# Measured durations and a DMA clock in a planner of instruction order, and block merges that alternate between halves of the TensorE array

## Chip, cores and metric

One Trainium2 chip, one core, one launch. The metric is the device time in microseconds (us) of the whole launch. Engines are named as in the profile: PE (TensorE), ACT (ScalarE), DVE (VectorE), POOL (GpSimd), SP (SyncE, which issues the DMAs).

## The reference

Two blocks of a sequence model on 512 tokens of width 2048, all in fp32. Block 1 projects the normed input, runs a gated delta rule of 24 heads in chunks, an attention of 4 heads over 256 memory tokens, gates the result and projects it back. Block 2 does the same with an mLSTM of 4 heads and an HGRN2 of 8 heads, then adds a gated embedding and norms the result. Cut to what matters here:

```python
def gated_delta_rule(q, k, v, g, beta):            # the heart of block 1
    decay = exp(where(incl, gc[..., :, None] - gc[..., None, :], -inf))
    m = where(strict, beta[..., :, None] * kk * decay, 0.0) + eye(C)
    sol = triangular_solve(m, rhs, lower=True, unit_diagonal=True)
    def step(state, inp):
        u = u0_c - w_c @ state
        o = qd_c @ state + qk_c @ u
        state = cd_c * state + kd_c.T @ u
...
mem_n = rms_norm(mem, mem_norm_g)
h = rms_norm(x, norm_g)
proj = h @ dn_w_in
xa = memory_cross_attention(xq, mem_n, mem_w_kv, ...)
x = x + (concat([deltanet(proj), xa]) * silu(z)) @ w_out
...
h = h + concat([mlstm(...), hgrn2(...)]) @ w_out_2
h = h + sigmoid(rmsnorm(h, pe_norm_w) @ w_pg) * (p @ w_pe)
out = rmsnorm(h, final_norm_w)
```

The kernel solves the triangular systems with an explicit inverse.

## The kernel before

**Products.** Activations lie transposed, as 16 tiles of 128 channels by 512 tokens. Weights come from HBM in pieces of four k-tiles (`raw`, 128x512, 256 KB, six buffers). ACT makes `hi`, the piece rounded to fp32r (a copy), DVE makes `lo = raw - hi`, and each 128x128 weight tile is then multiplied three times: hi by the activation's high part (`xh`, or `mh` for the memory), hi by its low part (`xl`, `ml`), lo by the high part. Each piece so feeds twelve matmuls into an accumulator `acc` (a bank of PSUM). A product with the memory has 256 columns, one with x 512. Some 11,000 of these matmuls are the bulk of the program; everything else is meant to run beside them.

**What sets the order.** All instructions are issued by a class `Driver`. It keeps a clock for each engine in a plan: every helper (`act`, `tt`, `stt`, `ts`, `cp`, `set`, `keep`, `scan`, `mm`, `dma`) issues an instruction and moves its engine's clock on by a cost that is written into the helper; a result counts as ready at `tau`, 0.3 us after that clock. Tasks (generators: one for each step of a head or group) go on when their `tau` is not later than PE's planned clock, and in between the driver issues the next unit of three weight matmuls, if its `lo` is planned to be ready. `_pump` issues the loads of weight pieces, the `hi` and the `lo` ahead. So the costs decide which instruction stands where in each engine's queue; on the chip, each queue runs strictly in this order.

**The start.** `first_loads` is called after each weight piece's load. It issues the eight memory tiles `mraw` with the first eight pieces, then the sixteen tiles `xraw` of x with the next sixteen. `mem_task` makes `mh` (ACT) and `ml` (DVE) for each memory tile, at a planned time of 3.8 + 1.5 i us. `x_task` squares each x tile (ACT, `xsq`) and adds it into `xsum` (DVE); the sum over partitions is a matmul `ss`, and x is then scaled, and split into `xh` and `xl`. The first jobs are the eight heads' pieces of w_k, two of them at a time, since a memory tile must have come before its matmuls.

**The inverse.** For each of twelve groups (two heads, four chunks of 128 tokens, so eight systems of 128) a task `inv` inverts the eight unit triangular matrices at once. The 32x32 diagonal blocks are done on DVE, row by row: for i in 1 to 31 a `tensor_tensor` product into `pr` and a `tensor_reduce` into column i of `Xb` (lines L131 and L881; both bear the name Xb, one buffer's). Then the blocks are merged on PE: `pp` and `px` (32x32 blocks), `p2` and `p3` (64x64 blocks; `p` in the trace), with the parts copied in between into `XT`, `XA` (the first 64x64 block's inverse, on partitions 0 to 63, eight of them side by side) and `P2`. All of p2's and p3's eight products write partitions 0 to 63.

**The recurrence.** Under the same matmuls, each group goes through four chunks: `ks` = S times the keys (PE), `rp` (DVE), `up` (PE), `u` (ACT) and `ud` (DVE), `pst` (PE), the new state `S` (DVE). DVE does the next group's inverse in between. `o` are the outputs.

**The end.** The last w_pg jobs run in two halves of 256 tokens. `evac_g` makes the gate `gt` (a sigmoid on ACT), the new h (`h1r`) and its sum of squares; `out_half` multiplies h by the final norm's weight and by 1/rms (`gt` again). Every third tile is scaled by the weight on ACT and then multiplied on POOL (`tt`), the others take one `stt` on DVE. A table of ACT functions is loaded when the function changes class (`ACT_TABLE_LOAD`).

Of the kernel before, what the change touches and what calls it, by code (L numbers as in the profile page):

```python
# [18 lines left out]
T = 512  # L19
# [59 lines left out]
class Driver:  # L79
# [5 lines left out]
    def __init__(self, tc, wp, psp, sp):  # L85
        self.tc, self.nc, self.wp, self.psp, self.sp = tc, tc.nc, wp, psp, sp
        self.clk = dict(pe=0.0, act=0.0, dve=0.0, pool=0.0)
# [13 lines left out]
        self.table = None  # L101
        self.nhead, self.head = 0, None
# [8 lines left out]
    def act(self, out, in_, func, table=None, **kw):  # L111
        t = table or {AF.Exp: 1, AF.Ln: 1, AF.Silu: 2, AF.Sigmoid: 3}.get(func)
        cost = 0.11 + free_size(out) / 1200
        if t and t != self.table:
            self.table = t
            cost += 1.3
# [18 lines left out]

    def ts(self, out, a, s1, op0, s2=None, op1=None, eng=None):
        kw = dict(op1=op1) if op1 is not None else {}
        self._v(eng, free_size(out)).tensor_scalar(out=out, in0=a, scalar1=s1, scalar2=s2, op0=op0, **kw)

    def cp(self, out, a, eng=None):  # L140
        self._v(eng, free_size(out)).tensor_copy(out=out, in_=a)

    def set(self, out, v, eng=None):
        self._v(eng, free_size(out)).memset(out, v)

    def keep(self, out, in_, sign, fill):
# [5 lines left out]
        self._on("pool", 0.2 + n * c / 1200, LV)  # L152

    def scan(self, out, a, b, init, op0, op1):
        self._v(None, free_size(out)).tensor_tensor_scan(out=out, data0=a, data1=b, initial=init, op0=op0, op1=op1)

    def mm(self, out, lhsT, rhs, start=True, stop=True, tr=False):
        n = free_size(out)
        if lhsT.dtype == F32R:
            c = max(0.107, n / 2400)  # L160
        elif tr:
            c = 0.105
        else:
            c = max(0.055 if lhsT.shape[0] <= 32 else 0.107 if lhsT.shape[0] <= 64 else 0.2, n / 600)
            if lhsT.shape[0] <= 64:
                c = min(c, 0.107)
# [99 lines left out]
    def _pump(self):  # L266
        while self.i_dma < len(self.pieces):
# [6 lines left out]
            self.pieces[self.i_dma] = (j, c0, n, raw, max(self.clk["pe"] + 3.0, 4.5 + 1.5 * self.i_dma))  # L274
# [121 lines left out]
def build(ctx: ExitStack, tc: tile.TileContext, A, out):  # L396
# [49 lines left out]

    def first_loads(i):

        if i < len(mraw):
            nc.sync.dma_start(out=mraw[i], in_=A["memT"][:, 2 * i:2 * i + 2])  # L450
        elif i < len(mraw) + KT:
            k = i - len(mraw)
# [4 lines left out]
            d.give(f_x[k])  # L457
            f_x[k].tau = d.clk["pe"] + 3.0

    f_x = [Fut() for _ in range(KT)]  # L460
# [99 lines left out]
    def mem_task():  # L560
        hs = []
        for i, t in enumerate(mraw):
            d.tau = 3.8 + 1.5 * i
# [27 lines left out]
    def x_task():  # L591
        ssum = yield from slot(name="xsum")
        for k, t in enumerate(xraw):
            yield from need(f_x[k])
            yield from d.calm(AHEAD)
# [6 lines left out]
            free(q)  # L602
        f = Fut()
# [135 lines left out]
    def evac_ab(job):  # L739
# [22 lines left out]
        d.dma(dgc, rows[0:32])  # L762
# [89 lines left out]
    def inverse(g, Mn):  # L852
# [24 lines left out]
        d._on("dve", 1.2, LV)  # L877
# [14 lines left out]
        XA = yield from slot((128, 8, 64), name="XA")  # L892
        d.set(XA[0:64], 0.0, pool)
# [10 lines left out]
        for b in range(4):  # L904
# [3 lines left out]
            if b < 2:  # L908
                act(XA[s, :, s], Dn[s], AF.Copy)
# [25 lines left out]
        cp(XA[32:64, :, 0:32], px[32:64, 0:8])  # L935
# [7 lines left out]
        p2 = p2_.rearrange("p (m c) -> p m c", c=64)  # L943
# [1066 lines left out]
```

## Time and profile before

| | us |
|---|---|
| median of 3 runs | 2913.86 |
| lowest, highest | 2908.96, 2915.22 |
| the profiled execution | 2909.13 |
| its span, first to last instruction | 2907.3 |
| PE busy | 2856.6 |
| DVE busy | 1722.0 |
| ACT busy | 1395.3 |
| POOL busy | 81.0 |

The profiled execution gives rows for every instruction: when it started, how long it took, and what the engine had waited for. Where PE is busy without a break, its busy time is the time; where it isn't, the row after the gap names what released it. A record's length on PE overlaps the next one's, so what a matmul costs is read from one start to the next. The granted clock is TensorE's, as a share of 2.4 GHz.

### The profile page before, as it was taken

Reading aid. Unit: us, or ns where it says so; the run is one execution under the profiler, and the core shown is the slowest. Engines: PE = TensorE matmul, PEld = TensorE weight load, DVE = VectorE, ACT = ScalarE, POOL = GpSimd, SP = SyncE. Lnnn points to the kernel's source line nnn. Section 1 sums busy time; section 2 is a strip of 40 time slices with the busy share of each in tenths; the row PEclk is TensorE's granted clock in tenths of the full one; section 3 lists DMA queues with packets and bytes.
Section 4 is the critical chain, followed back from the end, with each engine's and each line's share of the span. In section 5 each row is a group of like instructions: output and inputs, shape, how many; then the busy total and the mean of one; then the engine's idle time right before and its main releaser. Section 6 shows DMA issues by size and latency. Waiting matters only on the chain. (4 is left out here: it accounts for less than half of the span.)

```text
span 2907.3 us, 41141 instructions
## 1 busy us (share of the span) xinstructions
PE 2856.6 (98%) x15032; PEld 2390.5 (82%) x15032; DVE 1722.0 (59%) x3305; ACT 1395.3 (48%) x2636; POOL 81.0 (3%) x180
## 2 busy tenths in 40 slices
PE   8999999999999999999999999999999999999997
PEld 7877887788788888888888878888888888888887
DVE  6746677778777777635333364455655655544446
ACT  6544545555445555435222334445555556433434
POOL 0000100100000100000000000000000000000000
PEclk9999999999999999999999999999999999999999
DMA  7422422233222222354433433222222222333324
GB/s 244 142 80 93 123 93 90 95 101 96 82 93 99 95 98 92 100 168 129 129 118 120 148 110 109 87 81 80 84 80 80 89 86 87 115 119 112 96 94 145
DMA packets 179021, 311.05 MB, mean 107 GB/s; under 512 B 25345, under 2 KB 32129, under 8 KB 178817
## 3 DMA queue, kind: packets, MB, share of 16 engines
q1 hardware_dynamic: 178816, 308.41, 33.4%
q8 instruction: 118, 1.93, 0.3%
q14 instruction: 87, 0.70, 0.1%
HBM read 292.34 MB, written 15.99 MB: 106 GB/s over the span
## 5 line engine op out<-in xcount | busy, mean ns | idle before, releaser
L131 DVE TENSOR_TENSOR lo<-raw,hi 128x512 fp32r<-128x512 f32 (+1 forms) x956 | 643.9, 685 | 618.5 <-ACT hi L120 599.5
L120 ACT ACTIVATE hi<-raw 128x512 fp32r<-128x512 f32 (+1 forms) x964 | 591.6, 621 | 865.0 <-PE acc L167 761.8
L167 PE MATMUL acc<-xh,hi 128*128 128x512 f32 x1424 | 582.4, 409 | 0.7 <-ACT xh L120 0.4
L167 PE MATMUL acc<-xl,hi 128*128 128x512 f32 x1424 | 556.2, 391 | 2.8 <-DVE xl L131 2.7
L167 PE MATMUL acc<-xh,lo 128*128 128x512 f32 x1408 | 551.5, 392 | 4.5 <-DVE lo L131 4.4
L167 PE MATMUL acc<-x2h,hi 128*128 128x512 f32 x1040 | 415.8, 400 | 0.0
L167 PE MATMUL acc<-x2l,hi 128*128 128x512 f32 x1040 | 405.2, 390 | 0.0
L167 PE MATMUL acc<-x2h,lo 128*128 128x512 f32 x1024 | 399.8, 390 | 0.0
L167 PEld LDWEIGHTS acc<-xh,lo 128*128 128x128 f32 x1408 | 264.4, 188 | 63.7 <-DVE lo L131 6.2
L167 PEld LDWEIGHTS acc<-xl,hi 128*128 128x128 f32 x1424 | 268.5, 189 | 54.6 <-DVE xl L131 3.9
L167 PEld LDWEIGHTS acc<-xh,hi 128*128 128x128 f32 x1424 | 268.2, 188 | 53.6 <-issue 1.7
L167 PE MATMUL acc<-ph,hi 128*128 128x512 f32 x768 | 298.8, 389 | 0.0
L167 PE MATMUL acc<-pl,hi 128*128 128x512 f32 x768 | 298.8, 389 | 0.0
L167 PE MATMUL acc<-ph,lo 128*128 128x512 f32 x768 | 298.8, 389 | 0.0
L167 PEld LDWEIGHTS acc<-x2h,lo 128*128 128x128 f32 x1024 | 192.2, 188 | 41.4
L167 PEld LDWEIGHTS acc<-x2h,hi 128*128 128x128 f32 x1040 | 195.6, 188 | 37.2
L167 PEld LDWEIGHTS acc<-x2l,hi 128*128 128x128 f32 x1040 | 195.7, 188 | 36.9
L167 PEld LDWEIGHTS acc<-pl,hi 128*128 128x128 f32 x768 | 144.2, 188 | 30.0
L167 PEld LDWEIGHTS acc<-ph,hi 128*128 128x128 f32 x768 | 144.2, 188 | 29.9
L167 PEld LDWEIGHTS acc<-ph,lo 128*128 128x128 f32 x768 | 144.2, 188 | 29.8
L134 DVE SCALAR_TENSOR_TENSOR cv<-acc,c_dn_conv,cv 128x511 f32<-128x511 f32 x144 | 107.4, 747 | 35.6 <-ACT cv L120 32.1
L131 DVE TENSOR_TENSOR Xb<-Xb,Nb 128x16 f32<-128x16 f32 (+30 forms) x372 | 115.4, 310 | 8.8
(322 smaller groups left out, 3679.8 us busy)
## 6 DMA issues: line engine op xcount, KB each, us to landing
raw<-w_qkv SPq DMA_DIRECT2D x192, 256.0 KB, 3.2
raw<-w_out SPq DMA_DIRECT2D x192, 256.0 KB, 2.9
raw<-w_z SPq DMA_DIRECT2D x128, 256.0 KB, 3.2
raw<-w_pg SPq DMA_DIRECT2D x76, 256.0 KB, 3.1
gR<-dgc SPq DMA_DIRECT2D x48, 256.0 KB, 4.1
raw<-w_k SPq DMA_DIRECT2D x32, 256.0 KB, 4.7
raw<-w_v SPq DMA_DIRECT2D x32, 256.0 KB, 3.6
raw<-w_xq SPq DMA_DIRECT2D x32, 256.0 KB, 3.1
```

Source lines behind the costliest of these rows:

```text
L120: self.nc.scalar.activation(out=out, in_=in_, func=func, **kw)
L131: self._v(eng, free_size(out)).tensor_tensor(out=out, in0=a, in1=b, op=op)
L134: self._v(None, free_size(out)).scalar_tensor_tensor(out=out, in0=a, scalar=s, in1=b, op0=op0, op1=op1)
L167: self.nc.tensor.matmul(out, lhsT=lhsT, rhs=rhs, start=start, stop=stop, is_transpose=True if tr else None)
```

## The change

- **Costs.** The helpers' costs are set anew. ACT: 0.055 or 0.105 us by the source (PSUM or SBUF) instead of 0.11, and 0.075 more with a scale or bias from memory. DVE: 0.07 instead of 0.08 for `tt`, 0.13 for `stt`, half the time per element for copies and `ts` from SBUF, about double for `scan`. POOL: 0.43 + n/590 for a `tt` of n elements instead of 0.1 + n/400. PE: a 512-column fp32r matmul 0.227 instead of 0.213, and 0.15 for a change between small and full products. In the inverse, the big transpose 2.0 instead of 1.2, and the `tensor_reduce` 0.07 instead of 0.33 (+ elements/960 in both).
- **A DMA clock.** `land` plans when a load lands (clocks of SP's issue and of the DMA queue, 1.1 or 0.7 us for 256 KB); weight pieces, first loads and `dma` use it. `y_loader` no longer waits in the plan for its loads.
- **The start.** The memory and x tiles are spread over the first 49 pieces by a list `loads`; four w_k jobs are interleaved instead of two; `mem_task` and `x_task` wait for the planned landing; the sums `xsum` go from DVE to POOL.
- **The inverse.** p2 and p3 write the products of even and odd systems to partitions 0 to 63 and 64 to 127 in turn, in one half of the columns (128x256 instead of 64x512). `XA` is 128x4x64: it takes two more ACT copies and one more DVE copy. P2 is one copy of 128x256; p3 leaves by two ACT and two DVE copies instead of two ACT copies.
- **The end.** h is scaled by the weight on ACT for all tiles but the last three (nine scalings more); those tiles take a `tt`, on POOL for k = 1, 4, 7, 10 and now 12, on DVE for the others.

The core of the diff (the other costs are as told above):

```diff
-        cost = 0.11 + free_size(out) / 1200
+        cost = (0.055 if in_psum(in_) else 0.105) + free_size(out) / 1200
...
-            c = max(0.107, n / 2400)
+            c = max(0.107, (n + 32) / 2400)
...
-            d._on("dve", 0.33 + 8 * (i + 1) / 960, LV)
+            d._on("dve", 0.07 + 8 * (i + 1) / 960, LV)
...
+    def land(self, n=128 * T, extra=0.1):
+
+        t = max(self.clk["pe"], self.clk["sp"])
+        self.clk["sp"] = t + 0.5
+        self.dq = max(self.dq, t + 2.0)
+        self.dq += (0.7 if self.dq > 9 else 1.1) * n / (128 * T)
+        return self.dq + 0.25 + extra
...
+    loads = [[] for _ in range(1 + 3 * KT)]
+    for i in range(len(mraw)):
+        loads[4 * (i // 2) + (i % 2 if i < 2 else i % 2 - 1)].append(("m", i))
...
-                cp(ssum, q)
+                cp(ssum, q, eng=pool)
             else:
-                tt(ssum, ssum, q, ADD)
+                tt(ssum, ssum, q, ADD, eng=pool)
...
         for m in range(8):
-            mm(p2[0:64, m], Mn[m // 4][64:128, m % 4, 0:64], XT[m // 4][64:128, m % 4, 64:128])
-        act(P2[0:64], p2[0:64], AF.Copy)
+            o = slice(64 * (m % 2), 64 * (m % 2) + 64)
+            mm(p2[o, m // 2], Mn[m // 4][64:128, m % 4, 0:64], XT[m // 4][64:128, m % 4, 64:128])
+        act(P2h, p2, AF.Copy)
...
-            mm(p3[0:64, m], XA[0:64, m], P2[0:64, m])
+            o = slice(64 * (m % 2), 64 * (m % 2) + 64)
+            mm(p3[o, m // 2], XA[o, m // 2], P2h[o, m // 2])
...
-                if on_pool(i):
-                    act(h, h, AF.Copy, scale=w[:, i:i + 1])
+                act(h, h, AF.Copy, scale=w[:, i:i + 1])
...
-    d.add(jk[0], jk[1])
+    d.add(*jk[:4])
```

**Where instructions move.** First ACT's queue in the first microseconds, before: `hi` are weight pieces, `mh` the memory's high parts, `xsq` the squares of x.

```order
L120 ACTIVATE mh_214<-mraw_81,c_mem_norm_g_75 128x256 x2
L120 ACTIVATE hi_226<-raw_123 128x512
L120 ACTIVATE mh_242<-mraw_82,c_mem_norm_g_75 128x256 x2
L120 ACTIVATE xsq_248<-xraw_89 128x512
L120 ACTIVATE hi_257<-raw_126 128x512
L120 ACTIVATE mh_270<-mraw_83,c_mem_norm_g_75 128x256 x2
L120 ACTIVATE hi_282<-raw_154 128x512
L120 ACTIVATE xsq_286<-xraw_90 128x512
L120 ACTIVATE mh_289<-mraw_84,c_mem_norm_g_75 128x256 x2
L120 ACTIVATE hi_307<-raw_180 128x512
```

And after:

```order
L128 ACTIVATE hi_200<-raw_119 128x512
L128 ACTIVATE mh_211<-mraw_80,c_mem_norm_g_75 128x256 x2
L128 ACTIVATE hi_223<-raw_122 128x512
L128 ACTIVATE xsq_237<-xraw_89 128x512
L128 ACTIVATE hi_243<-raw_127 128x512
L128 ACTIVATE xsq_259<-xraw_90 128x512
L128 ACTIVATE hi_265<-raw_151 128x512
L128 ACTIVATE mh_276<-mraw_81,c_mem_norm_g_75 128x256 x2
L128 ACTIVATE hi_290<-raw_173 128x512
```

The first squares still stand between the weights' high parts, but there are fewer memory tiles ahead of them, and more weight pieces.

Then, later in the same queue of the changed kernel, the last squares of x, whose sums POOL makes now, up to the copy `qh` that takes the whole sum:

```order
L128 ACTIVATE xsq_886<-xraw_100 128x512
L128 ACTIVATE hi_892<-raw_821 128x512
L128 ACTIVATE xsq_902<-xraw_101 128x512
L128 ACTIVATE xsq_908<-xraw_102 128x512
L128 ACTIVATE hi_916<-raw_833 128x512
L128 ACTIVATE xsq_924<-xraw_103 128x512
L128 ACTIVATE hi_935<-raw_845 128x512
L128 ACTIVATE xsq_941<-xraw_104 128x512
L128 ACTIVATE qh_944<-xsum_134 128x512
```

Before, the sums stood in DVE's queue, each behind its square.

Second, DVE's queue in a recurrence step of block 1, before: from the new state `S` to `rp`, with six instructions of another group's inverse between them.

```order
L134 SCALAR_TENSOR_TENSOR S_8017<-S_7929,cd_6561,pst_8015 128x128 x2
L131 TENSOR_TENSOR sq_7605<-sq_7605,sz_7925 128x512
L131 TENSOR_TENSOR Xb_7590<-Xb_7590,Nb_7670 128x8x17
L881 TENSOR_REDUCE Xb_7590<-Xb_7590 128x8
L131 TENSOR_TENSOR Xb_7590<-Xb_7590,Nb_7670 128x8x18
L881 TENSOR_REDUCE Xb_7590<-Xb_7590 128x8
L131 TENSOR_TENSOR Xb_7590<-Xb_7590,Nb_7670 128x8x19
L881 TENSOR_REDUCE Xb_7590<-Xb_7590 128x8
L131 TENSOR_TENSOR ql_8030<-sq_8027,qh_8029 128x512
L131 TENSOR_TENSOR lo_8054<-raw_7864,hi_8052 128x512
L134 SCALAR_TENSOR_TENSOR rp_8081<-ks_8077,nbeg_3034,vb_7128 128x128
L134 SCALAR_TENSOR_TENSOR rp_8081<-ks_8077,nbeg_3034,vb_7135 128x128
```

After, in the step with the same part of an inverse:

```order
L143 SCALAR_TENSOR_TENSOR S_7703<-S_7607,cd_6834,pst_7701 128x128 x2
L140 TENSOR_TENSOR Xb_7551<-Xb_7551,Nb_7618 128x8x11
L927 TENSOR_REDUCE Xb_7551<-Xb_7551 128x8
L140 TENSOR_TENSOR Xb_7551<-Xb_7551,Nb_7618 128x8x12
L927 TENSOR_REDUCE Xb_7551<-Xb_7551 128x8
L140 TENSOR_TENSOR Xb_7551<-Xb_7551,Nb_7618 128x8x13
L927 TENSOR_REDUCE Xb_7551<-Xb_7551 128x8
L140 TENSOR_TENSOR lo_7719<-raw_7572,hi_7717 128x512
L143 SCALAR_TENSOR_TENSOR rp_7728<-ks_7724,nbeg_3000,vb_7427 128x128
L143 SCALAR_TENSOR_TENSOR rp_7728<-ks_7724,nbeg_3000,vb_7435 128x128
```

The same count of inverse instructions stands between `S` and `rp`. On PE, between `ks` and `up`, there were two `o`, fifteen `acc` and two `ss` before, and there are two `o` and six `acc` now.

Third, ACT's queue at the end, before: `gt<-ss` is the first half's 1/rms, the other `gt` are sigmoids.

```order
L120 ACTIVATE hi_25718<-raw_25658 128x512
L120 ACT_TABLE_LOAD
L120 ACTIVATE gt_25726<-gt_25726 128x256
L118 ACT_TABLE_LOAD
L120 ACTIVATE gt_25647<-ss_25736 128x256
L120 ACTIVATE gt_25647<-gt_25647 128x256
L120 ACTIVATE hi_25750<-raw_25666 128x512
L120 ACTIVATE hi_25764<-raw_25678 128x512
L120 ACTIVATE hi_25778<-raw_25742 128x512
L120 ACT_TABLE_LOAD
L120 ACTIVATE gt_25796<-gt_25796 128x256
```

After:

```order
L128 ACTIVATE hi_25769<-raw_25695 128x512
L128 ACTIVATE gt_25718<-ss_25773 128x256
L128 ACTIVATE gt_25718<-gt_25718 128x256
L128 ACTIVATE hi_25792<-raw_25700 128x512
L128 ACT_TABLE_LOAD
L128 ACTIVATE gt_25803<-gt_25803 128x256
L128 ACTIVATE hi_25821<-raw_25708 128x512
L128 ACTIVATE hi_25837<-raw_25729 128x512
L128 ACTIVATE hi_25853<-raw_25778 128x512
```

The square root's steps now stand ahead of the sigmoid, whose table is loaded once for what follows.

## Rows read from the trace of the kernel before

**Rows 1.** The head of the page and its busy times of the engines over the whole span (busy us, share of the span, instructions).

```profile
span 2907.3 us, 41141 instructions
...
PE 2856.6 (98%) x15032; PEld 2390.5 (82%) x15032; DVE 1722.0 (59%) x3305; ACT 1395.3 (48%) x2636; POOL 81.0 (3%) x180
```

**Rows 2.** The windows view by stage: the stretch, its length, then busy us (and instructions) of PE, PEld, DVE, ACT and POOL, the granted TensorE clock as a share of full speed, the DMA engines' busy share and GB/s. The stages are: memory keys and values; the begin of the projections of x; the inverses and recurrences of the delta rule, which run under the projections; the output projection of block 1; the mLSTM; the rest of block 2; the end.

```profile
0.00:122.00 122.00, 108.38 (x818) 105.97 (x819) 91.31 (x168) 80.35 (x155) 0.20 (x4) 0.96 0.66 215
122.00:132.00 10.00, 6.84 (x27) 4.44 (x26) 9.68 (x16) 5.24 (x9) 0.00 (x0) 1.00 0.19 63
...
292.00:1240.00 948.00, 935.70 (x5649) 775.93 (x5648) 712.51 (x1609) 512.73 (x1118) 69.90 (x156) 1.00 0.30 96
1240.00:1679.00 439.00, 439.00 (x1938) 363.55 (x1937) 168.06 (x258) 147.47 (x241) 0.00 (x0) 1.00 0.44 137
1679.00:1910.00 231.00, 225.81 (x1124) 189.63 (x1124) 120.52 (x192) 98.11 (x170) 2.95 (x4) 1.00 0.33 100
1910.00:2860.00 950.00, 950.00 (x4550) 794.36 (x4549) 509.46 (x852) 458.57 (x772) 1.75 (x8) 1.00 0.29 93
2860.00:2908.00 48.00, 30.92 (x248) 29.80 (x246) 33.21 (x69) 20.08 (x33) 6.14 (x8) 0.88 0.51 164
```

**Rows 3.** The view of waits of TensorE: who waited, for whom, us in total, times, the longest.

```profile
PE acc L167 <- ACT mh L120: 7.1, 1, 7.1
PE pst L167 <- DVE ud L131: 3.2, 1, 3.2
```

**Rows 4.** The windows view of the first 80 us in steps of 5 us, columns as in rows 2.

```profile
20.00:25.00 5.00, 5.00 (x24) 4.78 (x24) 4.89 (x11) 4.88 (x11) 0.00 (x0) 0.50 0.98 365
...
50.00:55.00 5.00, 5.00 (x31) 5.00 (x32) 4.70 (x10) 1.78 (x3) 0.00 (x0) 0.68 0.63 209
```

**Rows 5.** The timeline of 17 to 21 us, all engines: start us, length us, engine, line, operation, out<-in, how many in a row, and in brackets the engine's idle time before it and what ended it.

```profile
18.33 0.63 ACT L120 ACTIVATE xsq<-xraw 128x512 f32<-128x512 f32 x1 [3.51 <-DMA xraw<-xT]
...
19.53 0.58 PE L167 MATMUL acc<-mh,hi 128*128 128x256 f32 x1 [2.46 <-ACT hi L120]
```

**Rows 6.** The timeline of TensorE around three small products of one inverse (group 0): `pp` and `px` of 32 by 32 blocks, `p` of 64 by 64 blocks (the merge that the change calls p2; p3 bears the same name in the trace). Each fp32 product leaves two records.

```profile
388.25 0.69 PE L167 MATMUL pp<-Dt,gR 32*32 32x32 f32 x32
388.88 0.50 PE L167 MATMUL acc<-xh,hi 128*128 128x512 f32 x1
...
399.10 0.19 PE L167 MATMUL px<-Dt,P 32*32 32x32 f32 x1
399.12 0.20 PE L167 MATMUL px<-P,Dt 32*32 32x32 f32 x2
399.13 0.19 PE L167 MATMUL px<-Dt,P 32*32 32x32 f32 x1
399.25 0.50 PE L167 MATMUL acc<-xh,hi 128*128 128x512 f32 x1
...
400.83 1.14 PE L167 MATMUL p<-XT,gR 64*64 64x64 f32 x16
...
401.91 0.50 PE L167 MATMUL acc<-xh,hi 128*128 128x512 f32 x1
```

**Rows 7.** The view of lines of VectorE: groups with busy us, mean ns of one, and the idle time before them. The first two are the steps of the twelve inverses, the last the sums of squares of x.

```profile
L131 DVE TENSOR_TENSOR Xb<-Xb,Nb 128x16 f32<-128x16 f32 (+30 forms) x372 | 115.4, 310 | 8.8
L881 DVE TENSOR_REDUCE Xb<-Xb 128x8 f32<-128x16 f32 (+30 forms) x372 | 110.4, 297 | 12.8
...
L131 DVE TENSOR_TENSOR xsum<-xsum,xsq 128x512 f32<-128x512 f32 x15 | 10.3, 690 | 6.1 <-ACT xsq L120 5.9
```

**Rows 8.** The timeline of 780.5 to 784.7 us, inside one group's recurrence, with VectorE in the middle of the next group's inverse.

```profile
781.06 0.60 PE L167 MATMUL ks<-S,cv 128*128 128x256 f32 x2
...
781.34 0.25 DVE L881 TENSOR_REDUCE Xb<-Xb 128x8 f32<-128x96 f32 x1
781.50 0.61 PE L167 MATMUL o<-gR,S 128*128 128x128 f32 x4
781.63 0.27 DVE L131 TENSOR_TENSOR Xb<-Xb,Nb 128x104 f32<-128x104 f32 x1
...
781.86 0.47 PE L167 MATMUL acc<-xh,hi 128*128 128x512 f32 x1
...
782.11 0.60 DVE L134 SCALAR_TENSOR_TENSOR rp<-ks,nbeg,vb 128x128 f32<-128x128 f32 x2
```

**Rows 9.** The timeline of the last 30 us: the products that make the output tiles, first GpSimd's, then VectorE's. GpSimd's first four run while VectorE makes none, VectorE's first ten while GpSimd makes none; the last four and the last twelve run side by side.

```profile
2881.73 2.83 POOL L131 TENSOR_TENSOR out<-h1r,gt 128x256 f32<-128x256 f32 x4 [390.25 <-ACT gt L120]
2896.40 3.31 POOL L131 TENSOR_TENSOR out<-h1r,gt 128x256 f32<-128x256 f32 x4 [11.84 <-ACT gt L120]
...
2888.49 4.04 DVE L134 SCALAR_TENSOR_TENSOR out<-h1r,c_fin_w,gt 128x256 f32<-128x256 f32 x10
...
2896.35 6.80 DVE L134 SCALAR_TENSOR_TENSOR out<-h1r,c_fin_w,gt 128x256 f32<-128x256 f32 x12 [0.86 <-ACT gt L120]
```

**Rows 10.** The timeline of 1812 to 1816 us in the mLSTM: VectorE's convolution of the next head, and TensorE's wait.

```profile
1812.87 2.32 DVE L134 SCALAR_TENSOR_TENSOR mcv<-pr,c_ml_conv,mcv 128x511 f32<-128x511 f32 x3 [0.88 <-ACT mcv L120]
...
1815.77 0.49 PE L167 MATMUL num<-rowb,Cs 128*128 128x128 f32 x2 [2.14 <-DVE Cs L134]
```

**Rows 11.** The timeline of 2886 to 2888 us, in the last gate products: VectorE's low parts of the last weights, and TensorE's wait for them.

```profile
2886.69 1.89 DVE L131 TENSOR_TENSOR lo<-raw,hi 128x512 fp32r<-128x512 f32 x3
...
2887.43 0.38 PE L167 MATMUL acc<-x3h,lo 128*128 128x256 f32 x1 [1.98 <-DVE lo L131]
```

More of the change, by code (lines that the diff above doesn't have):

```diff
@@ L40, in v4, with in_psum @@
     return ap.rearrange("p (n c) -> p n c", n=NCH)
+def in_psum(ap):
+    return ap.tensor.space == "PSUM"
 def free_size(ap):
@@ L112, in act @@
         t = table or {AF.Exp: 1, AF.Ln: 1, AF.Silu: 2, AF.Sigmoid: 3}.get(func)
-        cost = 0.11 + free_size(out) / 1200
+        cost = (0.055 if in_psum(in_) else 0.105) + free_size(out) / 1200
+        if not all(isinstance(kw.get(k, 0.0), (int, float)) for k in ("scale", "bias")):
+            cost += 0.075
         if t and t != self.table:
             self.table = t
-            cost += 1.3
+            cost += 1.29
             if t == 1:
@@ L151, in keep @@
             compare_op=ALU.is_ge if sign > 0 else ALU.is_gt, fill=fill)
-        self._on("pool", 0.2 + n * c / 1200, LV)
+        self._on("pool", 0.1 + n * c / 1050, LV)
     def scan(self, out, a, b, init, op0, op1):
-        self._v(None, free_size(out)).tensor_tensor_scan(out=out, data0=a, data1=b, initial=init, op0=op0, op1=op1)
+        self._v(None, 0.07 + free_size(out) / 460, 0).tensor_tensor_scan(
+            out=out, data0=a, data1=b, initial=init, op0=op0, op1=op1)
     def mm(self, out, lhsT, rhs, start=True, stop=True, tr=False):
         n = free_size(out)
+        small = max(lhsT.shape[0], free_size(lhsT)) <= 64
         if lhsT.dtype == F32R:
-            c = max(0.107, n / 2400)
+            c = max(0.107, (n + 32) / 2400)
         elif tr:
-            c = 0.105
-        else:
-            c = max(0.055 if lhsT.shape[0] <= 32 else 0.107 if lhsT.shape[0] <= 64 else 0.2, n / 600)
-            if lhsT.shape[0] <= 64:
-                c = min(c, 0.107)
+            c = 0.109
+        elif small:
+            c = 0.035 if lhsT.shape[0] <= 32 else 0.11
+        else:
+            c = max(0.222, (n + 5) / 600)
+        if small != self.small_mm:
+            self.small_mm = small
+            c += 0.15
         self.nc.tensor.matmul(out, lhsT=lhsT, rhs=rhs, start=start, stop=stop,
@@ L273, in _pump @@
             self.nc.sync.dma_start(out=raw[:, :n, :j.w.shape[2]], in_=j.w[:, c0:c0 + n])
[L274 removed]
+            self.pieces[self.i_dma] = (j, c0, n, raw, self.land(n * 128 * j.w.shape[2]))
             self.i_dma += 1
@@ L445, in build @@
         xraw.append(d.slot_now(name="xraw"))
-    def first_loads(i):
[L449 to L452, printed above, removed]
+    loads = [[] for _ in range(1 + 3 * KT)]
+    for i in range(len(mraw)):
+        loads[4 * (i // 2) + (i % 2 if i < 2 else i % 2 - 1)].append(("m", i))
+    n = 0
+    for i in range(len(loads)):
+        if n < KT and (i % 4 in (1, 2) and i > 4 if i < KT else i >= KT):
+            loads[i].append(("x", n))
+            n += 1
+    def first_loads(i):
+        for what, k in loads[i] if i < len(loads) else ():
+            if what == "m":
+                nc.sync.dma_start(out=mraw[k], in_=A["memT"][:, 2 * k:2 * k + 2])
+                f_m[k].tau = d.land()
+                f_m[k].done = True
+                continue
             if k == 0:
@@ L456, in first_loads @@
             nc.sync.dma_start(out=xraw[k], in_=A["xT"][:, k])
-            d.give(f_x[k])
-            f_x[k].tau = d.clk["pe"] + 3.0
+            f_x[k].tau = d.land(extra=0.5)
+            f_x[k].done = True
+    f_m = [Fut() for _ in mraw]
     f_x = [Fut() for _ in range(KT)]
@@ L562, in mem_task @@
         for i, t in enumerate(mraw):
-            d.tau = 3.8 + 1.5 * i
+            d.tau = 0.0
+            yield from need(f_m[i])
             yield
@@ L579, in mem_task @@
             d.tau = t0
+            yield from need(f_m[i])
             yield from d.calm(AHEAD)
@@ L761, in evac_ab @@
         yield
-        d.dma(dgc, rows[0:32])
+        d.dma(dgc, rows[0:32], n=32 * T)
         pt = yield from transpose4(rows)
@@ L891, in inverse @@
             XT.append(t)
-        XA = yield from slot((128, 8, 64), name="XA")
-        d.set(XA[0:64], 0.0, pool)
+        XA = yield from slot((128, 4, 64), name="XA")
+        d.set(XA, 0.0, pool)
         Dd = yield from slot((128, 2, 8, 32), name="Dt")
@@ L949, in inverse @@
         p3_ = yield from bank("p3")
-        p3 = p3_.rearrange("p (m c) -> p m c", c=64)
+        p3 = p3_[:, :256].rearrange("p (m c) -> p m c", c=64)
         for m in range(8):
-            mm(p3[0:64, m], XA[0:64, m], P2[0:64, m])
+            o = slice(64 * (m % 2), 64 * (m % 2) + 64)
+            mm(p3[o, m // 2], XA[o, m // 2], P2h[o, m // 2])
+        t1 = d.tau
         for hh in range(2):
-            act(XT[hh][0:64, :, 64:128], p3[0:64, 4 * hh:4 * hh + 4], AF.Copy)
+            act(XT[hh][0:64, 0::2, 64:128], p3[0:64, 2 * hh:2 * hh + 2], AF.Copy)
+        t2 = d.tau
+        d.tau = t1
+        for hh in range(2):
+            cp(XT[hh][0:64, 1::2, 64:128], p3[64:128, 2 * hh:2 * hh + 2])
+        d.tau = max(d.tau, t2)
         d.free_bank()
@@ L1691, in on_pool @@
     def on_pool(k):
-        return k % 3 == 1 and k < KT - NSP
+        return k % 3 == 1 and k < KT - NSP or k == KT - NSP - 1
     def evac_g(i):
@@ L1756, in build @@
     d.head = first_loads
-    d.nhead = len(mraw) + KT
+    d.nhead = len(loads) - 1
     d.spawn(mem_task(), 1)
@@ L1761, in build @@
     jv = [Job(A["w_v"][e], M, evac_v(e), NM) for e in range(2 * XH)]
-    d.add(jk[0], jk[1])
-    for j in jk[2:] + jv[:-2]:
+    d.add(*jk[:4])
+    for j in jk[4:] + jv[:-2]:
         d.add(j)
```

62 lines of the change are left out of this document (40 added, 22 removed).

## The prediction, made before the changed kernel ran

> **What bounds the kernel now.** I read first the busy times of the page: PE is busy 2856.6 of 2907.3 us, 98% [rows 1]. So 50.7 us of the span are not PE's, and only three things can move the time: these gaps, stretches of PE at a lower clock, and PE work that gets shorter. DVE (59%), ACT (48%) and POOL (3%) matter only where PE waits for them. Then I read the windows by stage [rows 2]. PE stands 122 - 108.38 = 13.6 us in the first stage, of which 7.1 are the wait for the first `mh` [rows 3], so 6.5 later; 10 - 6.84 = 3.2 where the x projections begin; 948 - 935.70 = 12.3 under the inverses; 5.2 in the mLSTM; 17 at the end, most of it after the last matmul. The outputs of blocks 1 and 2 show no gap at all (439.00 of 439, 950.00 of 950). Third, the clock: 0.50 at 20 to 25 us, just after PE had stood 2.46 us, and 0.68 at 50 to 55 [rows 4, 5]; these two windows cost 2.5 + 1.6 = 4.1 us. Last, the small products, whose price the timeline shows [rows 6].
>
> **The merges (TensorE's own work).** `p` holds PE from 400.83 to 401.91, the start of the next `acc`: 1.08 us for 16 records; about 0.12 of it is the way out (px: last record 399.13, next `acc` 399.25), so 0.96, or 60 ns a record, all in one place of the array. `pp` alternates between two places: 0.63 - 0.12 = 0.51 us for 32 records, 16 ns each, so the same place comes again after 32 ns; `px` has three places, 0.03 us from one `Dt,P` record to the next, so three records in the time of one place [rows 6]. That is half of 60 for blocks of half the columns, so I take a place's own time as the price and the other places as free. p2 and p3 in two places then take 0.48 instead of 0.96, in 12 groups x 2 merges: 24 x 0.48 = **-11.5 us**. The bounds are 0 (no overlap) and -11.5; if one of the two overlaps, -5.8. p2's two places share rows and differ in columns, as two of px's do; p3's differ in both, as pp's do.
>
> The Trainium skill, TensorEngine Tiling (Array Packing), section Restrictions and Gotchas, says that different row tiles cannot use the same PSUM bank at the same time. By that rule p3 would stay serial and the sum would have -5.8 here; pp, whose two row groups write one bank 16 ns apart [rows 6], speaks against it for small blocks, and no row shows it for 64x64.
>
> The copies around the merges cost no PE time: two ACT copies and one DVE copy more for `XA`, two DVE copies more behind p3, fewer columns in P2. They lie under ACT's and DVE's free time in 292 to 1240 us (513 and 713 of 948 busy [rows 2]); uncovered they would delay a merge that waits anyway, under 0.5 us a group, and that is within the term for that stage.
>
> **The start.** PE's 2.46 us gap at 19.53 follows `xsq`, at which ACT had stood 3.51 us for x's DMA with the weights' `hi` queued behind it [rows 5]. After, the plan knows landings, and four jobs share each memory tile: a piece of 262 KB feeds twelve 256-column matmuls of 0.12 us, 1.4 us, or 182 GB/s, and the memory's 2 MB are wanted over twice as many pieces, so 91 GB/s instead of 182 beside the weights; the DMA moved 365 GB/s where PE had work [rows 4]. Of the 6.5 us I take **-4**, bounds 0 and -6.5: `xsq` still stands between `hi` copies. The clock's 4.1 us followed the gaps, so I take **-3**, bounds 0 and -4.1.
>
> **The begin of x.** DVE is busy 9.68 of 10 us while PE stands 3.2 [rows 2]; the work (`stt`, `xl`, `lo`) is the same, the plan now prices the `stt` rightly and so can begin earlier. **-1.5**, bounds 0 and -3.2.
>
> **xsum on POOL.** DVE loses 15 sums, 10.3 us [rows 7], which no row shows PE waiting for. POOL has no 512-column `tt` in the trace; four of 256 columns alone take 2.83 us, 0.71 each [rows 9], so one takes 0.71 to 1.42. Eight stand in a burst before `qh`, and behind `qh` the weights' `hi`. Eight at 1.42 are 11.4 us, against 8 x 1.30 = 10.4 in the plan, and DVE slows where POOL works: ten `out` alone take 4.04, 0.40 each, while twelve beside POOL's four take 6.80 instead of 4.85, so some 0.5 us for each POOL `tt` [rows 9]. If `qh` comes late, ACT stands, and PE after it. I take **+2**, bounds 0 and +5.
>
> The Trainium skill, SBUF — State Buffer, on the shared port pair, has it that DVE with two SBUF inputs and POOL exclude each other for a whole instruction. The rows agree in sign (1.95 us for four POOL products), and the price above is the rows'.
>
> **The recurrences under the inverse.** DVE's steps of an inverse take (115.4 + 8.8 + 110.4 + 12.8) / 12 = 20.6 us a group [rows 7]. The old costs gave 31 x 0.41 + 8.8 = 21.5, the new give 31 x 0.14 + 8.8 = 13.1 (0.07 twice; the elements add 8.8 either way). This "measured" price is 7.5 us short for each inverse, so the plan puts too much into DVE between the links of a recurrence. In the step shown of the order after, `rp` comes after six Xb instructions (0.29 each [rows 8], 1.75), one `lo` (0.60) and itself (0.60): 2.95 us after S. PE has in that time `ks` (781.06 to 781.50, 0.44), `o` (0.36) [rows 8] and six `acc` of 439.00/1938 = 0.227 [rows 2]: 2.16. So PE stands some 0.8 us there. Before, fifteen `acc` and two `ss` (17 x 0.227) make that 4.7, against 2.95 and two more DVE operations, 4.2: no wait. The other three links of that group, reckoned the same way, give 0.6, so 1.4 a group; over the ten groups with this pattern 14 us, against 12.3 now, which had other causes (`ud` 3.2 [rows 3]) and mostly vanish: **+2**. Bounds -12.3 (no wait left) and +48 (5 us of the 7.5 exposed in each of twelve).
>
> **The mLSTM.** PE stood 2.14 us for `Cs`, which stood behind three convolution steps [rows 10], 2.32 us that the old plan priced 3 x 0.61 and the new 3 x 0.66. **-3** of 5.2, bounds 0 and -5.2.
>
> **The end.** The 1.98 us gap for `lo` [rows 11] came from low parts that stood behind two gate chains with table loads between; now one chain stands ahead, and a load less. The last twelve `stt` take 6.80 us [rows 9]; after, DVE has eleven, eight as `tt`, at most 0.40 each, with five POOL products beside them: 4.4 + 5 x 0.5 = 6.9, so nothing. **-2**, bounds -4 and +1. Nine ACT scalings more lie in 1910 to 2860 us (ACT 459 of 950, PE without a gap [rows 2]): nothing. Seven table loads fewer, off PE's path: nothing.
>
> **Sum.** -11.5 - 4 - 3 - 1.5 + 2 + 2 - 3 - 2 = -21.0, against the profiled execution's 2909.13: 2888.1. That execution is near the lowest of the three runs and 4.7 us under their median, 2913.86; I add 2 for that: **2890**, some 0.8% under the median.
>
> **Rivals.** (a) *The underpriced inverse decides* and it is slower: if 5 of the 7.5 missing us stand on PE's path in each of twelve groups, the stage has 60 us of gaps instead of 14, so 2936. It takes from 3.2 us a group to give the whole gain back (38 us of gaps). For it: `pst` waited 3.2 for `ud` under a plan that had the price right. Against: between links PE has enough weight matmuls, and the order shows the same six Xb instructions a link as before. (b) *The merges do not do what they say*: 2890 + 11.5 = 2901.5 if no place overlaps, 2896 if only p2 does, the skill's rule. (c) *The sums on POOL* stop `qh`, ACT and PE at the end of the start, and the clock falls as at 20 us: +8, 2898. (d) *All gaps that the plan sees go*, the middle's too: 14 + 2.5 + 2 less, 2872.
>
> **Chances.** Forecast 0.60, (a) 0.12, (b) 0.10, (c) 0.10, (d) 0.08. A measurement of this kernel tells some 0.2%, 5.8 us, from no change: faster is under 2908. The forecast, (b), (d) and six in ten of (c) are: 0.60 + 0.10 + 0.08 + 0.06 = 0.84. (a) holds 0.07 of slower; its milder half, with the bad end of (c), 0.05 + 0.04 = 0.09 of no change. The range goes from (d) to where the gain is all but gone, 2871 to 2908: it leaves out (a) and the far ends, under 0.2.
>
> **What would show it.** Right: `p` rows of about 0.6 us; PE busy some 11 us less; the gap near 19 us gone and no 0.50 window; gaps in 292 to 1240 us of about 14, at `ks`, `up` or `pst` for DVE, one pattern per group. Wrong: `p` rows of 1.1; PE waiting for `rp` or `ud` over 3 us a group; a gap for `qh` or `hi` at the end of xsum; VectorE's records stretched beside POOL's sums.

## The result and the profile after

The changed kernel takes 2949.18 us (median of 4 runs, 2947.68 to 2949.73) against 2914.54 for the kernel before: 1.24% slower, ratio 1.0124 (95% interval 1.0109 to 1.0139). 2890 was forecast, with a range of 2871 to 2908. The sign was wrong.

The windows by stage, columns as in [rows 2], with the stretches moved to the same places of the program (the third begins at the same time and ends where the output projection, which has no gap in either kernel, is well under way):

```profile
0.00:122.00 122.00, 106.15 (x790) 104.05 (x791) 87.11 (x158) 81.12 (x157) 21.40 (x20) 0.93 0.64 208
122.00:132.00 10.00, 10.00 (x49) 8.27 (x48) 5.25 (x10) 3.75 (x7) 0.00 (x0) 1.00 0.42 136
...
292.00:1273.00 981.00, 935.72 (x5607) 757.99 (x5606) 711.57 (x1639) 509.20 (x1138) 64.45 (x156) 0.99 0.29 92
...
1722.00:1953.00 231.00, 227.56 (x1142) 191.81 (x1141) 122.28 (x195) 99.70 (x173) 2.85 (x4) 1.00 0.33 102
...
2902.00:2946.00 44.00, 30.23 (x244) 29.31 (x242) 33.53 (x67) 17.18 (x31) 8.80 (x10) 0.88 0.54 177
```

Under the inverses PE now stands 981 - 935.7 = 45.3 us, where it stood 12.3 [rows 2]. The begin of x has no gap (3.2 before), the mLSTM 3.4 (5.2). The whole loss is in the third stretch and, less, in the first, whose clock is 0.93 (0.96 before). TensorE's waits, as in [rows 3]:

```profile
PE pst L186 <- DVE ud L140: 15.5, 18, 2.5
PE pp L186 <- issue: 7.5, 9, 1.0
PE ss L186 <- ACT qh L128: 6.8, 3, 4.4
...
PE p L186 <- DVE XA L154: 5.0, 2, 3.7
...
PE ks L186 <- DVE S L143: 4.4, 8, 0.8
...
PE up L186 <- DVE rp L143: 1.1, 3, 0.6
```

`pst` for `ud` was one wait of 3.2 and is eighteen, 15.5 us; `ks` for `S` is new. The wait of `pp` that the view calls "issue" ends with the last transpose of the inverse on DVE: the timeline of 890 to 893 us shows one, and the seven last groups have one each, 0.8 to 1.0 us.

```profile
891.55 0.45 DVE L947 STREAM_TRANSPOSE Dt<-Dt 128x256 f32<-128x256 f32 x1
...
892.10 0.69 PE L186 MATMUL pp<-Dt,gR 32*32 32x32 f32 x32 [1.01 <-issue]
```

From 892 us on, the pattern comes again every 86 us, a group each: `pp` 1.0, `pst` 1.1, `ks` 0.6, and smaller ones. Inside it, DVE is busy without a break while PE waits for the new state:

```profile
949.99 0.31 DVE L140 TENSOR_TENSOR Xb<-Xb,Nb 128x144 f32<-128x144 f32 x1
950.33 0.30 DVE L927 TENSOR_REDUCE Xb<-Xb 128x8 f32<-128x144 f32 x1
950.67 0.32 DVE L140 TENSOR_TENSOR Xb<-Xb,Nb 128x152 f32<-128x152 f32 x1
951.02 0.31 DVE L927 TENSOR_REDUCE Xb<-Xb 128x8 f32<-128x152 f32 x1
951.25 0.68 DVE L140 TENSOR_TENSOR lo<-raw,hi 128x512 fp32r<-128x512 f32 x1
951.85 0.60 DVE L143 SCALAR_TENSOR_TENSOR S<-S,cd,pst 128x128 f32<-128x128 f32 x2
...
951.37 0.39 PE L186 MATMUL acc<-xl,hi 128*128 128x512 f32 x1
951.60 0.39 PE L186 MATMUL acc<-xh,lo 128*128 128x512 f32 x1
952.60 0.67 PE L186 MATMUL ks<-S,cv 128*128 128x256 f32 x2 [0.61 <-DVE S L143]
```

A pair of inverse steps takes 0.68 us here (949.99 to 950.67); the plan has 0.14 + 2 x 8 x 18/960 = 0.44 (the old costs gave 0.41 + 0.30 = 0.71). Three such pairs and a `lo` stand between the `ud` that let `pst` start and `S`.

A gap is not all that a wait costs. `ks` shows a gap of 0.61 behind the record of `acc` that starts at 951.60. But two `acc` start 0.23 apart (951.37, 951.60), and `ks` starts 1.00 after the last one: it is 0.77 late, since a record of 0.39 us runs on beyond the point where the next could have started. So the loss is larger than the gaps. From the first product of x to the first one of block 2, which is the same work in both kernels, the windows are (first the kernel before, then the changed one):

```profile
116.63:1687.20 1570.57, 1555.11 (x8362) 1281.91 (x8361) 974.86 (x2040) 743.72 (x1519) 69.90 (x156) 1.00 0.34 106
...
122.26:1730.33 1608.07, 1562.79 (x8362) 1271.52 (x8361) 968.39 (x2061) 737.52 (x1535) 64.45 (x156) 1.00 0.33 104
```

That is 37.5 us more: 29.8 of gaps (45.3 against 15.5), and 7.7 of PE's busy time, which by the shorter merges alone would have fallen by some 10.

The merges did what was forecast. The timeline of group 0, as in [rows 6]:

```profile
392.81 0.68 PE L186 MATMUL p<-XT,gR 64*64 64x64 f32 x16
393.42 0.50 PE L186 MATMUL acc<-xh,hi 128*128 128x512 f32 x1
...
453.24 0.68 PE L186 MATMUL p<-P,XA 64*64 64x64 f32 x16 [1.24 <-ACT P L128]
453.86 0.50 PE L186 MATMUL acc<-xh,hi 128*128 128x512 f32 x1
```

0.61 us from `p` to the next `acc`, for p2 (`XT,gR`) and, in group 1, for p3 (`P,XA`), where p2 took 1.08 [rows 6]. Of the 24 merges 21 take 0.61, the other three 0.69 to 1.27.

The sums of squares on POOL, and who waits for them (POOL, ACT and PE in turn; then the windows of 5 us):

```profile
63.90 11.12 POOL L140 TENSOR_TENSOR xsum<-xsum,xsq 128x512 f32<-128x512 f32 x8 [15.69 <-ACT xsq L128]
...
75.05 0.63 ACT L128 ACTIVATE qh<-xsum 128x512 fp32r<-128x512 f32 x1 [6.09 <-POOL xsum L140]
...
75.73 0.80 PE L186 MATMUL ss<-qh,ones_r 128*128 128x512 f32 x1 [4.42 <-ACT qh L128]
...
70.00:75.00 5.00, 1.32 (x12) 1.11 (x10) 0.00 (x0) 0.00 (x0) 4.77 (x4) 0.97 0.00 0
75.00:80.00 5.00, 4.27 (x16) 3.73 (x17) 3.23 (x7) 2.47 (x6) 0.02 (x1) 0.50 0.29 90
```

ACT stands 6.09 us for the eighth sum, all its weights' `hi` behind it; PE stands 4.42, and is granted half the clock in the next 5 us.

### The profile page after: what moved, and what is told of

The parts are those of the page before. It is cut to its first block, busy times and chain, and to the rows that moved or that the text cites. A ratio compares the mean times of both kernels' runs of the same rounds, so it can differ in the third digit from the quotient of the medians.

```text
span 2945.9 us, 41214 instructions
## 1 busy us (share of the span) xinstructions
PE 2867.3 (97%) x15032; PEld 2383.1 (81%) x15032; DVE 1716.2 (58%) x3323; ACT 1389.8 (47%) x2662; POOL 99.0 (3%) x198
## 5 line engine op out<-in xcount | busy, mean ns | idle before, releaser
L143 DVE SCALAR_TENSOR_TENSOR cv<-acc,c_dn_conv,cv 128x511 f32<-128x511 f32 x144 | 107.6, 747 | 34.3 <-ACT cv L128 30.6
```

The lines of the kernel that those rows point to most:

```text
L143: self._v(None, 0.13 + free_size(out) / 960, 0).scalar_tensor_tensor(out=out, in0=a, scalar=s, in1=b, op0=op0, op1=op1)
```

## The experiments

The kernel before ran beside each batch, with medians of 2911 to 2912; ratios are to it. "us" are medians.

**The two suspects, each way.** The edits:

```diff
-            d._on("dve", 0.07 + 8 * (i + 1) / 960, LV)      # after_reduce_price_back, on the changed kernel
+            d._on("dve", 0.33 + 8 * (i + 1) / 960, LV)
...
-            d._on("dve", 0.33 + 8 * (i + 1) / 960, LV)      # before_reduce_price_new, on the kernel before
+            d._on("dve", 0.07 + 8 * (i + 1) / 960, LV)
...
-                cp(ssum, q, eng=pool)                        # after_xsum_on_dve, and the tt after it
+                cp(ssum, q)
```

Expected of after_reduce_price_back: 

> The changed kernel with one number set back: the plan's cost of the inverse's tensor_reduce is 0.33 us again instead of 0.07 (its tensor_tensor keeps the new 0.07, so a pair costs 0.40 plus the elements, about what the trace shows). Theory A (the underpriced inverse puts too many DVE steps between the links of the recurrence, and PE waits for ud, S and rp): the waits of pst, ks, up and pp under the inverses fall from some 35 us to under 10, and the time falls from 2949 to about 2905 to 2915. Theory B (other new prices, as those of stt, copies, POOL or the small products, move the recurrence): the waits stay, 2940 to 2950.

Measured: 2922.5, ratio 1.0039 (1.0026 to 1.0051): 27 us faster than the changed kernel. `pst`'s waits are 11.3 us, those of `ks` for `S` and of `pp` for "issue" are no longer among the eleven longest. The price was the main cause, but 7 to 17 us more than expected stay. The gaps from 292 us on are 973 - 943.8 = 29.2 us: `pst` still waits 11.3 (3.2 in the kernel before), and p3 waits four times for `XA`, 8.0 us (2.5 before).

Expected of before_reduce_price_new: 

> The kernel before with that one number changed: 0.07 instead of 0.33 for the tensor_reduce. Theory A: it alone makes the waits, 30 to 45 us slower, 2945 to 2960. Theory B: within 5 us of 2914.

Measured: 2938.3, ratio 1.0093 (1.0077 to 1.0108): the one number makes the kernel before 27 us slower, somewhat less than expected. `pst` waits 7 times instead of once; the last line is the window of the inverses:

```profile
PE pst L167 <- DVE ud L131: 6.9, 7, 3.0
...
PE ks L167 <- DVE S L134: 2.5, 7, 0.4
PE up L167 <- DVE rp L134: 2.5, 6, 0.6
PE pp L167 <- DVE Dt L900: 2.2, 5, 0.5
...
292.00:1267.00 975.00, 949.78 (x5645) 773.71 (x5644) 707.84 (x1611) 515.88 (x1121) 69.70 (x156) 1.00 0.29 93
```

Against the 948 and 935.7 of [rows 2] that is 27 us more for as many matmuls: 12.9 of gaps, and 14.1 of busy time. PE has 41 gaps there instead of 13; at 0.16 each, as at `ks` above, 28 more hide an estimated 4.5 us in busy time. What makes up the rest of the 14 is not shown.

Expected of after_xsum_on_dve: 

> The changed kernel with the sums of squares of x on DVE again. If POOL's sums make the 4.4 us wait of ss and the low clock after it, the first stage gets 5 to 8 us shorter, 2941 to 2944; if the new order of the loads alone makes them, under 2 us.

Measured: 2939.3, ratio 1.0095 (1.0080 to 1.0110), 9.8 us faster than the changed kernel, more than the 5 to 8 expected; in its first 122 us PE is busy 111.66 instead of 106.15 at a clock of 0.99 instead of 0.93:

```profile
0.00:122.00 122.00, 111.66 (x841) 108.28 (x842) 99.41 (x183) 85.23 (x164) 0.20 (x4) 0.99 0.68 219
```

The whole of it lies in the first stage; the stage of the inverses has gaps of 981 - 937.0 = 44 us as with POOL's sums.

**Both undone.** after_reduce_back_xsum_dve: 

> The changed kernel with both suspects undone: the tensor_reduce at 0.33 us in the plan, the sums of squares of x on DVE. If the two are independent: 2949 - 27 - 10 = 2912. If the new order under the inverses is again one of chance: 2905 to 2922.

Measured: 2915.9, ratio 1.0015 (1.0006 to 1.0025). The two add up to within 4 us (2949.2 - 26.7 - 9.8 = 2912.6). Each has a second pair by this run: the price is worth 23.4 us with the sums on DVE (2939.3 to 2915.9), and the sums 6.6 us with the old price (2922.5 to 2915.9). But then the start, the end and the merges should leave a gain, and none is left. The same window as above shows where it went:

```profile
112.01:1697.99 1585.98, 1555.33 (x8363) 1276.53 (x8361) 975.21 (x2067) 742.09 (x1538) 63.95 (x156) 0.99 0.33 105
```

The first product of x comes 4.6 us earlier than in the kernel before (112.0, 116.6), and from block 2 to the end it takes 1215.4 us instead of 1220.2: these gains are there. Between the two it takes 15.4 us longer, 30.6 of gaps instead of 15.5, and PE's busy time has not fallen by the merges' 11 us.

**The merges alone.** before_merges_alternate: 

> The kernel before with the merges alone changed (two places in turn, the copies that go with them, the costs as before). The merges' rows in the trace of after are 0.46 us shorter each, 24 of them: about 11 us, 2903. If the saved TensorE time comes back as waits, as it would where VectorE's chain is the limit, 2908 to 2914.

Measured: 2914.8, ratio 1.0013 (1.0004 to 1.0022): nothing of the 11 us. The merges are as short as in after, and waits took their place (p3 for `XA` three times, 7.2 us). To take the new order out of it, the plan was charged as if nothing had changed:

```diff
-                act(XA[s, :, s], Dn[s], AF.Copy)
+                nc.scalar.activation(out=XA[s, :, s], in_=Dn[s, 0::2], func=AF.Copy)
+                nc.scalar.activation(out=XA[64 + 32 * b:96 + 32 * b, :, s], in_=Dn[s, 1::2], func=AF.Copy)
+                d._on("act", 0.11 + 256 / 1200, LV)
```

merges_order_held: 

> The kernel before with the merges alone changed, and the plan charged as if they were not: the new copies are issued, but the plan's clocks move by the old copies' costs, so that all other instructions stand in the order of before. Theory A (the merges save their 0.46 us each, 24 of them, and in the run before_merges_alternate the gain was lost to a new order): the waits are those of before, 2900 to 2904. Theory B (TensorE was not the limit around the merges, a chain of VectorE and ScalarE copies is, now longer by the extra copies): waits grow by what the merges save, 2909 to 2915.

Measured: 2926.5, ratio 1.0053 (1.0038 to 1.0068), slower, by waits that this edit made: `up` stood for `XT` six times, 0.6 to 2.5 us, since a copy of p3 on DVE stood in DVE's queue behind the next inverse's first steps, and ACT's second copy stood behind it (3.4 us at 486). So the run does not judge the merges; merges_held_copies_on_act does: 

> As merges_order_held, but all four copies of p3 on ScalarE; there the second ScalarE copy stood 3.4 us behind VectorE's first one, which stood in VectorE's queue. Theory A (the merges are worth their 11 us where no copy goes into VectorE's long queue): 2900 to 2904, and no wait of up for XT. Theory B (the merges' saving is not TensorE's to have, since its next work comes no earlier): 2909 to 2915.

Measured: 2911.3, ratio 0.9999 (0.9989 to 1.0008): no gain, at the order of before. The two traces can be laid side by side, matmul by matmul. The lead grows by 0.9 us at each group's merges and is lost again between them, part of it at waits. One of them, p3's for `XA`, in this kernel and in the one before (timeline of TensorE):

```profile
844.87 0.84 PE L167 MATMUL p<-P,XA 64*64 64x64 f32 x15 [2.04 <-DVE XA L938]
```

```profile
845.62 1.05 PE L167 MATMUL p<-P,XA 64*64 64x64 f32 x15 [1.32 <-DVE XA L141]
```

PE came to this wait 1.5 us earlier and left it 0.76 earlier: the gap is longer by half of the lead. At 1000.43 the same wait is 1.91 instead of 1.17, and the matmuls behind it start 0.43 apart instead of 0.23; the granted clock, last column but two of the window, is 0.60 there, while the kernel before has 1.00 at the same place (3.97 us busy of 4, 1002 to 1006 us). The lead there is 2.05 us before the wait, 1.59 behind it, and 0.42 four us later. The last two lines are the kernel before:

```profile
1000.43 0.95 PE L167 MATMUL p<-P,XA 64*64 64x64 f32 x16 [1.91 <-DVE XA L938]
...
1002.33 0.63 PE L167 MATMUL acc<-xh,lo 128*128 128x512 f32 x1
1002.76 0.63 PE L167 MATMUL acc<-xh,hi 128*128 128x512 f32 x1
...
1000.40:1004.70 4.30, 4.26 (x27) 3.54 (x27) 2.58 (x10) 1.09 (x4) 0.00 (x0) 0.60 0.53 176
...
1002.03 1.11 PE L167 MATMUL p<-P,XA 64*64 64x64 f32 x16 [1.17 <-DVE XA L141]
...
1002.00:1006.00 4.00, 3.97 (x31) 3.50 (x32) 2.67 (x10) 1.03 (x3) 0.00 (x0) 1.00 0.63 189
```

This is not one place alone. The mean granted clock of the ten executions is 0.9936, and 0.9953 in the fifteen of the kernel before beside them. (1 - clock) x span, an estimate of what the lower clock costs, is 18.6 us against 13.8. So the lower clock took some 4.8 of the 11 us; in the two traces the gaps took 3.2 more (18.7 against 15.5, from the first product of x to block 2).

**What a new order does by chance.** plan_latency_031_vector (`LV, LP = 0.31, 0.3`): 

> The kernel before with a number that means nothing for the chip: the planned latency of ScalarE, VectorE and GpSimd results is 0.31 us instead of 0.30. It shows how much any new order changes the time. Theory A (an order that the plan makes anew costs or gains some 10 us of waits by chance): 2900 to 2930, with the waits at other places. Theory B (small shifts of the plan do nothing): within 3 us of 2912.

plan_latency_031_tensor (`LV, LP = 0.3, 0.31`): 

> As plan_latency_031_vector, with the planned latency of TensorE results at 0.31 us instead of 0.30. Theory A: 2900 to 2930, other places again. Theory B: within 3 us of 2912.

Measured: 2915.0 (1.0016, 1.0006 to 1.0025) and 2910.2 (1.0000, 0.9990 to 1.0009): 4 us and nothing, with the waits at other places. The 4 us are no larger than what the clock took: by the same estimate 19.5 us at a mean of 0.9933, against 14.1 at 0.9952 beside it.

**The price of the matmul.** The edit is `c = max(0.107, (n + 32) / 2400)` for `n / 2400`, or back. before_matmul_price_new: 

> The kernel before with one price of the new ones: a 512-column fp32r matmul 0.227 us in the plan instead of 0.213 (the trace shows 0.227 to 0.229). Theory C (the old plan thought TensorE faster than it is, so that the other engines' queues had 6% of slack on the chip, and the right price takes it away): waits under the inverses grow by 10 to 25 us, 2920 to 2935. Theory A2 (only prices of other engines matter, a truer TensorE price gives a better order): 2905 to 2915.

Measured: 2893.3, ratio 0.9939 (0.9924 to 0.9954): theory C fails, the truer price gains 18 us. after_both_matmul_price_back: 

> The run after_reduce_back_xsum_dve (2916) with the 512-column matmul at 0.213 us in the plan again. Theory C: 10 to 25 us faster, 2890 to 2906. Theory A2: no faster than 2912.

Measured: 2902.4, ratio 0.9969 (0.9957 to 0.9980): 13 us faster than with the true price, as theory C had it. The two contradict each other, so neither theory stands. Three runs asked whether these are draws. matmul_price_new_latency_031: 

> The kernel before with the matmul at 0.227 us in the plan (2893) and the planned latency of ScalarE and VectorE at 0.31 us instead of 0.30. If the truer price is worth its 18 us whatever else the plan draws: 2888 to 2898. If the order was a lucky draw: 2900 to 2915.

before_matmul_price_220 (`(n + 16) / 2400`): 

> The kernel before with the matmul at 0.220 us, half way. If the truer price is worth its gain, in between or as good: 2890 to 2903. If it is a draw: anything from 2893 to 2920.

after_both_latency_031: 

> The run after_reduce_back_xsum_dve (2916) with the planned latency of ScalarE and VectorE at 0.31 us. If that order's waits belong to its prices: 2911 to 2921. If it was an unlucky draw: 2895 to 2908.

Measured: 2900.7 (0.9959, 0.9944 to 0.9974), 2911.0 (0.9996, 0.9986 to 1.0006) and 2904.3 (0.9973, 0.9963 to 0.9983). A latency that means nothing costs the good order 7 us and gains the bad one 12; half the price change does nothing. So a shift of up to some 12 us after any edit of the plan says nothing of the edit.

**Merges in other orders.** new_price_and_merges, the matmul price of 0.227 with the held merges, copies on ScalarE: 

> The kernel before with the matmul price of 0.227 us (as before_matmul_price_new, 2893) and the merges in two places, the plan charged as if they were unchanged, all copies of p3 on ScalarE (as merges_held_copies_on_act). Theory D (the merges' gain is given back at the next wait for another engine, so it is worth the more the fewer waits the order has; this order has about 8 us less of them under the inverses): 5 to 11 us faster than 2893, 2882 to 2888. Theory E (the lead always comes back, since VectorE and ScalarE pace every group): 2891 to 2895.

Measured: 2887.8, ratio 0.9921 (0.9906 to 0.9935), 5.6 us faster than without the merges, in an order that is the same but for them. Half of the 11 us stays there. This order had fewer waits (948 - 941.5 = 6.5 us of gaps in 292 to 1240), and here the clock hardly falls: 0.9958 with the merges and 0.9960 without, so 12.3 us against 11.6 by the estimate above. It is the fastest kernel of the study, 0.8% under the one before.

after_both_old_merges: 

> The run after_reduce_back_xsum_dve (2916) with the merges of before, in one place, with their copies. If the copies of the new merges (three more on VectorE in each group, in its queue between the inverse's steps) cost what TensorE saves: 2905 to 2917. If the merges bring their 11 us there: 2925 to 2929.

old_prices_new_structure: 

> The changed kernel's start, DMA clock, merges and end, the sums of squares on DVE, with all prices of the kernel before but the 512-column matmul's, 0.227. If the other new prices are what is left of the loss (waits of pst for ud and of p3 for XA): 2880 to 2893. If it is the structure: 2900 to 2916.

Measured: 2903.3 (0.9973, 0.9962 to 0.9984) and 2903.2 (0.9975, 0.9964 to 0.9985). Without the new merges the kernel with both undone is 12.6 us faster, and its gaps between the first product of x and block 2 are 15.3 us, as in the kernel before; with the old prices it is 12.7 faster. Both are no larger than a draw (after_both_latency_031 has the same 2904), so the two are not told apart.

**One more pair for the reduce price.** matmul_and_reduce_price_new, both edits on the kernel before: 

> The kernel before with the matmul at 0.227 us in the plan (2893) and the tensor_reduce at 0.07. If the underpriced inverse costs its 27 us in any order: 2912 to 2928. If the two pairs before were draws: 2883 to 2905.

Measured: 2960.0, the median of four executions, ratio 1.0169 (1.0152 to 1.0186): 67 us slower than with the old reduce price, the largest step of the study. The fifth execution, the profiled one, took 12.7 ms and is left out, so no trace stands behind this run.

## Why the prediction was wrong

**The step that failed** is the term for the recurrences under the inverse, +2: "1.4 a group; over the ten groups with this pattern 14 us, against 12.3 now". The gaps there are 45.3 us, +33. The mechanism was found and named (rival (a), a plan that has an inverse 7.5 us too short); its size was not. The reckoning took the four links of one group by DVE's instructions between `S` and `rp`, and took the other groups as alike. The wait that it priced, `up` for `rp`, came three times, 1.1 us in all. PE stood at other points of the loop instead: at `pst` for `ud` (15.5), at `ks` for `S` (4.4), and at `pp`, at the end of the inverse's chain (7.5), which the reckoning left out. In the groups from 892 us on the gaps add up to 3.2 us each, not 1.4. Against rival (a) stood "the same six Xb instructions a link as before"; what counts is the PE work between the links, and that had fallen from fifteen `acc` to six in the step shown, as the prediction's own sum said. (The two steps shown in the order are not the same part of an inverse: columns 17 to 19 before, 11 to 13 after.)

The pairs show the price itself as the main cause: 27, 27, 23 and 67 us, in four different kernels and always in the same direction, where meaningless shifts moved the time by up to 12 and the matmul's price by 18 one way and 13 the other. It is not all of the term: with the price back, 29.2 of the 45.3 us of gaps are left, 17 more than before the change, at `pst` and p3; what makes these is not told apart.

**The merges.** The price was right: 1.08 - 0.61 = 0.47 us each, 11.3 for all 24, so the sum's -11.5 was TensorE's saving to within 0.5 us at the full clock. The rule of the Trainium skill (TensorEngine Tiling (Array Packing), Restrictions and Gotchas) that different row tiles cannot access the same PSUM bank at a time did not keep p3 serial here: one at 453.24 us in the trace of after holds PE 0.61 us to the next `acc`, as p2 does. What failed is that shorter PE work was counted as time, one for one, with the gaps and the clock left as they were. A gap of 1.3 us is also a place where PE is paced by another engine, and can take back part of what PE saved before it; and behind a longer gap the clock can fall. Measured worth: 0 at the order of before, 5.6 us in an order with half the gaps, with the order held in both. Without the estimated cost of the clock it is about 6 us in both (2889.9 against 2895.7, 2873.6 against 2879.8), so that the second order kept its gain because it had fewer gaps is not shown; what differs is that its clock did not fall.

**xsum on POOL.** +2 was taken and +5 was the bound; undoing it gains 9.8 us, or 6.6 with the old reduce price. The single sum was priced right (0.71 to 1.42; the burst of eight takes 11.12, 1.39 each), and so was the place. Against the plan's own 10.4 for the eight that is 0.7 us late, but ACT stood 6.09; why the plan had nothing else to queue there is left open. Rival (c), the sums stop `qh`, ACT and PE and the clock falls, had the course of it and, at +8, nearly the size.

**Start, x, mLSTM and end.** With the sums on DVE, the last memory product comes 5.3 us earlier than in the kernel before (111.2 instead of 116.5), of the 7 forecast for idle time and clock; the begin of x lost its 3.2 (1.5 forecast); the mLSTM 1.8 of 5.2 (3 forecast); the last gate products and the output 3.0 (2 forecast). These were right within 2 us each.

**What stays open.** The 27 and 10 us account for the loss of 35 against 2914. With both undone, the gains of the start and the end are in the trace, and the recurrences take them back: 15 us more of gaps, and a merges' saving that does not show. Whether the new merges' copies in DVE's queue or the other new prices make these gaps is not told apart, since both effects are of the size of a draw. What the matmul's price is worth by itself is open for the same reason.

## What to carry to other kernels

Where a plan decides the order, a price that is too low on the engine that feeds the critical loop (here 0.07 each for two operations that take 0.19 each and their elements) can outweigh every other edit: check the sum of a chain of dependent small operations against the trace, not the price of one. An engine that is 98% busy is not yet the bound: what it saves can be lost at its next wait, or to a lower clock behind that wait, so read whether the waits come once or once per group, and the granted clock with them. The sum of the gaps understates what waits cost: compare starts over the same work. Before a gain of 0.4% is put down to an edit of a plan, shift the plan by something meaningless and see how much that moves.

## What was not expected of the hardware

One and the same place of the program had TensorE's granted clock at 0.60 behind a gap of 1.91 us, and at 1.00 behind one of 1.17: the merges of that group had saved 0.9 us, and 1.6 of the lead was lost there. A 512-column `tensor_tensor` on POOL, the mean of fifteen, took 1.37 us, near the upper of the two bounds that the 256-column rows gave.
